# A hybrid decoder step on one core: the z and gate projections move to a first phase done by Strassen's algorithm, and the SSD decay is clamped with Relu

## The chip, the cores and the metric

The kernel runs on one core of one Trainium2 chip. The core has a matrix engine (TensorE, PE in the rows; its weight loads are listed apart as PEld), a vector engine (DVE), an activation engine (ACT), a general engine (POOL) and a sync engine (SP), which here issues every DMA. The five run their own instruction queues in order and meet through semaphores. The metric is the device time of one launch in microseconds. A difference of 0.2% or less is what a measurement of this kernel can't tell from no change.

## The reference

One layer of a hybrid decoder, for 2048 prompt tokens and 64 sample tokens (8 sequences of 8), in float32. Cut to what matters here:

```python
h = rms_norm(x, norm_w)                               # (tokens, 1024)
q, k, v, z_a, z_s, xbc, dt, g = split(h @ w_in)       # 1024, 256, 256, 1024, 2048, 3072, 32, 2*1024 columns
o_a = window_attention(rope(norm(q)), rope(norm(k)), v, sinks)
a_cs = cumsum(dt * A); seg = a_cs[l] - a_cs[s]
Lm = exp(where(causal, seg, -inf))                    # the SSD decay matrix, 128 x 128 per head and chunk
o_s = grouped_rms((ssd(conv(xbc), Lm) + D * x) * silu(z_s))
merged = sigmoid(g_a) * ((o_a * silu(z_a)) @ w_attn) + sigmoid(g_s) * (o_s @ w_ssd)
y = x + merged @ w_out
```

The columns of `w_in` that this case is about are z_a (1024), z_s (2048) and the two gates (2048): 5120 of the 9760 columns.

## The kernel before

Every large product is computed with float32 split into two float32r parts, high and low: the high part is a copy on ACT (line 147) and the low part is the difference on DVE (line 148). A product then takes three matmuls, high*high, high*low and low*high (`SPLIT3`). Weights come from DRAM as a `raw` tile of 256 columns (1 MB) and are split into `whl`; the normed input, transposed, is `hT`, eight tiles of 128 model dims. One such weight tile against 512 tokens is 2 x 8 x 3 = 48 matmuls of 128x512.

The tokens go in four blocks of 512 (`TB`). The 64 sample tokens ride along with one block: its columns are 576, done as two halves of 288 (`proj_w`, line 181).

There are three stages, one after the other, each with its own pools:

- `phase_t1`, the attention stage. `prep_first` and `prep_h` load x, norm it, transpose it and write both parts to DRAM (`h_d`). For every block: z_a tiles (`za_tile`, matmuls on line 168), k, v and q tiles (line 192), then 32 attention units over all blocks (scores on line 519, transposes on 536, the product with v on 547).
- `phase_s`, the SSD stage. For every block and each of four groups, `proj_group` computes B, C, x (with the convolution, lines 739 to 753) and z_s (lines 814 and 815, with silu). Then `ssd_group` goes through four chunks of 128 tokens: the decay `L` (eight DVE subtract-and-min on line 843, one Exp on line 844, a POOL product on line 845), the matmuls `py`, `st` and `po`, the state `H`, and at last the product with `zs`. The tiles of `proj_group` have two sets, so that it can run one group ahead.
- `phase_t2`, the output stage, in block order 3, 0, 1, 2. `gate` computes tanh of the gate projections (line 1175); `w_ssd`, `w_attn` and `w_out` follow. `phase_sa` and `phase_ss`, the sample tokens' attention and SSD (the loop over their states is on lines 1073 to 1085), are emitted into the first block; the third block, which carries the sample columns, needs their results.

The order on each engine isn't the order of the code: a scheduler that keeps its own estimate of the time interleaves the instructions, so projections stand between the steps of attention and of the SSD chunks. PE runs whatever order that gave, in order.

Of the kernel before, what the change touches and what calls it, by code (L numbers as in the profile page):

```python
# [9 lines left out]
F32 = mybir.dt.float32  # L10
# [65 lines left out]
def build(tc, nc, a, o, seq, phases=("T1", "S", "T2"), dbg=None):  # L76
# [14 lines left out]
    h_d = [[dt_(f"h_d{b}_{k}", [P, 4, 2, TB]) for k in range(KT // 4)] for b in range(NB)]  # L91
# [9 lines left out]
    zs_d = dt_("zs_d", [P, 16, 64])  # L101
# [4 lines left out]
    zss_d = dt_("zss_d", [P, 8, 64])  # L106

    def dump(name, t):
        if dbg is not None and name in dbg:
            SY.dma_start(dbg[name], t)  # L110
# [144 lines left out]
    def prep_first(xp, jp, zap, trp):  # L255
        rows = jp.tile([KT, P], F32, name="rows", tag="rows")
        zz = zap.tile([P, HG, TB], F32, name="zs", tag="zs").rearrange("p (i c) t -> p i (c t)", i=2)
        xts = [xp.tile([P, D], F32, name="xt", tag="xt") if tt < 2 else zz[:, tt - 2] for tt in range(NT)]
        for tt, xt in enumerate(xts):
            SY.dma_start(xt, a["x_prompt"][0, tt * P : (tt + 1) * P, :])  # L260
        SY.dma_start(rows, a["norm_w"][0].rearrange("(c p) -> c p", p=P))
        ips = trp.tile([P, KT], F32, name="tr", tag="tr")
        PE.transpose(ips, rows, ident[:KT, :KT])
        nw = jp.tile([P, KT], F32, name="nw", tag="nw")
        V.tensor_copy(nw, ips)
        for xt in xts:
            norm_x(xt, jp, None)
        hT = []
        for k in range(KT):
            tp = trp.tile([P, TB], F32, name="tr", tag="tr")  # L270
            for tt in range(NT):
                PE.transpose(tp[:, tt * P : (tt + 1) * P], xts[tt][:, k * P : (k + 1) * P], ident)
            ht = cur["h"].tile([P, 2, TB], F32R, name="hT", tag="hT")
            A.activation(ht[:, 0], tp, AF.Identity, bias=0.0, scale=nw[:, k : k + 1])
            V.scalar_tensor_tensor(
                out=ht[:, 1], in0=tp, scalar=nw[:, k : k + 1], in1=ht[:, 0].bitcast(F32),
                op0=ALU.mult, op1=ALU.subtract,
            )
            SY.dma_start(h_d[0][k // 4][:, k % 4], ht.bitcast(F32))
            hT.append(ht)  # L280
        return hT

    def prep_h(b, xp, jp, trp, nwb):
        for tt in range(NT):
            ts = slice(tt * P, (tt + 1) * P)
            xt = xp.tile([P, D], F32, name="xt", tag="xt")
            SY.dma_start(xt, a["x_prompt"][0, b * TB + tt * P : b * TB + (tt + 1) * P, :])
            norm_x(xt, jp, nwb)
            for kh in range(2):
                tp = trp.tile([P, 4, P], F32, name="tr", tag="tr")  # L290
                for k in range(4):
                    c = (4 * kh + k) * P
                    PE.transpose(tp[:, k], xt[:, c : c + P], ident)
                st = xp.tile([P, 2, 4, P], F32R, name="hst", tag="hst", bufs=2)
                split(st[:, 0], st[:, 1], tp)
                for i in range(2):
                    SY.dma_start(h_d[b][kh][:, :, i, ts], st[:, i].bitcast(F32))

    def prep_s(xp, jp, trp, nwb):
        xsm = xp.tile([64, D], F32, name="xsm", tag="xt")  # L300
        SY.dma_start(xsm, a["x_sample"].rearrange("b t d -> (b t) d"))
        norm_x(xsm, jp, nwb, 64)
        tp = trp.tile([P, KT, 64], F32, name="tr", tag="tr")
        for k in range(KT):
            PE.transpose(tp[:, k], xsm[:, k * P : (k + 1) * P], ident[:64, :64])
        V.tensor_copy(hs, tp)
# [65 lines left out]

    def phase_t1():
        with ExitStack() as es:
# [6 lines left out]
            jp = pool("jp", 1)  # L381
# [24 lines left out]

            def za_tile(b, pair, hgp, hT, zs):
                raw, hl = wtile(za_parts(pair, hgp))
                r5 = raw.rearrange("p k (v h d) -> p k v h d", v=2, h=2)
                for hgl in range(2):  # L410
                    ov = [hl[:, i, :, hgl * P : hgl * P + P].rearrange("p k (v d) -> p k v d", v=2) for i in range(2)]
                    split(ov[0], ov[1], r5[:, :, :, hgl, :])
                for hgl in range(2):
                    ps = mmp.tile([P, TB], F32, name="mm", tag="mm")
                    proj_cm(ps, hl, hgl * P, hT)
                    th = wk.tile([P, TB], F32, name="th", tag="th", bufs=1)
                    A.activation(th, ps, AF.Tanh, scale=0.5)
                    V.scalar_tensor_tensor(  # L418
                        out=zs[:, 2 * hgp + hgl], in0=th, scalar=1.0, in1=ps, op0=ALU.add, op1=ALU.mult
                    )  # L420
                if b == sb:
                    pss = mmp.tile([P, P], F32, name="mm", tag="mm")
                    proj_s(pss, raw, hs, views=lambda k, half: r5[:, k, :, half, :])
                    zt = wk.tile([P, P], F32, name="zt", tag="zt", bufs=1)
                    V.tensor_copy(zt, pss)
                    tp = trp.tile([P, P], F32, name="tr", tag="tr")
                    PE.transpose(tp, zt, ident)
                    A.activation(zt, tp, AF.Tanh, scale=0.5)
                    V.scalar_tensor_tensor(out=zt, in0=zt, scalar=1.0, in1=tp, op0=ALU.add, op1=ALU.mult)
                    ct = pair * 4 + hgp * 2  # L430
                    SY.dma_start(zss_d[:, ct : ct + 2].rearrange("p c t -> p (c t)"), zt)
# [138 lines left out]
            nxt = prep_first(xp, jp, zap, trp)  # L570
            for b in range(NB):
# [3 lines left out]
                for pair in range(2):  # L575
                    zs = zap.tile([P, HG, TB], F32, name="zs", tag="zs")
                    if pair == 0:
# [6 lines left out]
                    if pair == 0 and b + 1 < NB:  # L584
                        prep_h(b + 1, xp, jp, trp, nwb)
                        if b + 1 == sb:
                            prep_s(xp, jp, trp, nwb)
                    if pair == 1:
                        for hgp in range(2):
                            za_tile(b, pair, hgp, hT, zs)  # L590
# [5 lines left out]
    def phase_sa(oas):  # L596
        with ExitStack() as es:
# [11 lines left out]
            SY.dma_start(zss, zss_d)  # L609
# [96 lines left out]
    def phase_s():  # L706
        with ExitStack() as es:
# [3 lines left out]
            cur["whl"], cur["w"] = pool("whl2", 2), 256  # L711
            pst = pool("pst", 1)
# [70 lines left out]
            def proj_group(b, g, hT):  # L783
# [23 lines left out]
                for i in range(2):  # L807
                    c = 512 * g + 256 * i
                    _, hl = wload([(0, w_in[:, OFF_ZS + c : OFF_ZS + c + 256])])
                    st = sample_tile(smp)  # L810
                    for j in range(2):
                        th = cp.tile([P, TB], F32, name="th", tag="th")
                        for ps, lo, n in prompt_pieces(proj_w(mmp, hl, j * P, hT, smp), st[:, j] if smp else None):
                            A.activation(th[:, lo : lo + n], ps, AF.Tanh, scale=0.5)
                            V.scalar_tensor_tensor(
                                out=zs[:, 2 * i + j, lo : lo + n], in0=th[:, lo : lo + n], scalar=1.0, in1=ps,
                                op0=ALU.add, op1=ALU.mult,
                            )
# [498 lines left out]
```

## Time and profile before

| | |
|---|---|
| time, median of 3 runs | 3273.84 us (3271.09 to 3276.58) |
| span of the profiled execution | 3273.9 us, the same as the median to 0.1 us |
| PE busy | 3130.4 us, 96% |
| DVE, ACT, POOL busy | 2234.8, 1308.2, 1045.0 us |
| attention stage | about 0 to 790 us |
| SSD stage | about 790 to 2063 us |
| output stage | about 2063 to 3274 us |

The profiled execution has no time of its own beside its span, from the first to the last instruction. Busy time on PE counts a matmul from its start to its modelled end; matmuls overlap, so the mean duration of one (396 ns for 512 columns) is longer than the distance from one to the next. Where a group is busy without a gap, its busy time divided by its count is what one matmul costs.

### The profile page before, as it was taken

The page shows a single profiled execution, that of the slowest core. Times are in us where ns is not written, and L with a number is a line of the kernel's source. Part 1 is how long each engine was busy: PE and PEld are TensorE (multiplying, and loading weights), DVE is VectorE, ACT ScalarE, POOL GpSimd, SP SyncE. Part 2 cuts the span into 40 slices and gives each one's busy share as a digit, 9 for nine tenths or more (in the row PEclk, how much of TensorE's full clock was granted, in tenths as well). Part 3 has the DMA queues.
Part 4 walks back from the last instruction along what each step waited for, and adds up shares of the span by engine and source line. Part 5 has one row for each costly group of instructions (what it writes and reads, how often), then busy time and mean ns, then how long its engine had stood idle before and what let it go on. Part 6 is the DMA issues. An engine that isn't in the chain of part 4 may idle for free.

```text
span 3273.9 us, 49350 instructions
## 1 busy us (share of the span) xinstructions
PE 3130.4 (96%) x19038; PEld 2656.9 (81%) x19038; DVE 2234.8 (68%) x3777; ACT 1308.2 (40%) x2334; POOL 1045.0 (32%) x965
## 2 busy tenths in 40 slices
PE   6999999999989999998999999999999999999999
PEld 5978787878878877776777777788877799999888
DVE  3777768678887798989888898555555554334433
ACT  3555535456344344434444444332333333222322
POOL 1534343443445455556554555200211110000000
PEclk8999999999999999999999999999999999999999
DMA  6544425323433444444344433444764574345443
GB/s 210 156 134 124 128 73 169 106 70 124 130 122 110 154 125 135 126 156 133 116 143 155 127 118 119 154 141 117 229 184 142 131 226 147 97 135 168 132 116 101
DMA packets 472788, 448.76 MB, mean 137 GB/s; under 512 B 33808, under 2 KB 420520, under 8 KB 472504
## 3 DMA queue, kind: packets, MB, share of 16 engines
q1 hardware_dynamic: 472552, 445.60, 44.9%
q8 instruction: 150, 2.46, 0.3%
q14 instruction: 86, 0.70, 0.1%
HBM read 382.26 MB, written 65.35 MB: 137 GB/s over the span
## 4 chain that ended last, share of the span: by engine, by line
PE 63%; DVE 24%; DMA 5%; POOL 3%; issue 3%; ACT 2%; SPq 1%; DVEq 0%; ACTq 0%; POOLq 0%
PE mm L181 37%; PE mm L192 11%; DVE acc L748 5%; DVE L L843 5%; PE mm L168 5%; DVE whl L148 3%; PE tr L547 3%; PE sc L519 2%; POOL L L845 2%; DVE zs L885 1%; DMA v<-v_d 1%; PE tr L536 1%; DVE xT L882 1%; DVE H L879 1%; DMA hT<-h_d 1%
## 5 line engine op out<-in xcount | busy, mean ns | idle before, releaser
L181 PE MATMUL mm<-hT,whl 128*128 128x512 f32 (+1 forms) x6720 | 1353.7, 357 | 19.8 <-DMA hT<-h_d 9.9
L181 PEld LDWEIGHTS mm<-hT,whl 128*128 128x128 f32 x6720 | 1122.0, 190 | 194.0 <-issue 22.9
L148 DVE TENSOR_TENSOR whl<-raw,whl 128x2048 fp32r<-128x2048 f32 (+1 forms) x232 | 522.7, 2256 | 261.7 <-ACT whl L147 255.4
L181 PE MATMUL mm<-ot,whl 128*128 128x512 f32 (+1 forms) x2880 | 571.7, 356 | 1.2 <-DVE whl L148 0.8
L181 PEld LDWEIGHTS mm<-ot,whl 128*128 128x128 f32 x2880 | 476.1, 189 | 74.0 <-issue 5.7
L147 ACT CAST whl<-raw 128x2048 fp32r<-128x2048 f32 (+1 forms) x232 | 412.7, 1787 | 250.1 <-PE mm L181 133.9
L192 PE MATMUL mm<-whl,hT 128*128 128x256 f32 (+1 forms) x2304 | 305.6, 288 | 16.2 <-ACT whl L147 12.8
L192 PEld LDWEIGHTS mm<-whl,hT 128*128 128x128 f32 x2304 | 288.6, 190 | 24.4 <-ACT whl L147 13.0
L748 DVE SCALAR_TENSOR_TENSOR acc<-cr,cwb,acc 128x512 f32<-128x512 f32 x288 | 274.9, 960 | 10.4 <-ACT acc L743 5.0
L845 POOL TENSOR_TENSOR L<-L,cbm 128x1024 f32<-128x1024 f32 x64 | 200.2, 3138 | 115.3 <-DVE cbm L834 57.9
L192 PE MATMUL mm<-whl,ot 128*128 128x256 f32 (+1 forms) x1632 | 203.9, 284 | 0.0
L192 PEld LDWEIGHTS mm<-whl,ot 128*128 128x128 f32 (+1 forms) x1632 | 197.6, 188 | 5.3 <-issue 4.9
L168 PE MATMUL mm<-hT,whl 128*128 128x512 f32 x768 | 195.1, 403 | 6.0 <-DVE zs L418 3.7
L843 DVE TENSOR_SCALAR L<-AB,acs 128x128 f32<-128x128 f32 x512 | 192.0, 443 | 0.0
L168 PEld LDWEIGHTS mm<-hT,whl 128*128 128x128 f32 x768 | 142.6, 191 | 42.0 <-issue 5.2
L844 ACT ACTIVATE L<-L 128x1024 f32<-128x1024 f32 x64 | 67.8, 1062 | 187.8 <-DVE L L843 187.8
L365 ACT ACTIVATE s<-s,ng 128x128 f32<-128x128 f32 x256 | 100.0, 394 | 59.9 <-DVE ng L359 57.7
L147 ACT CAST ot<-v 128x512 fp32r<-128x512 f32 x96 | 59.0, 621 | 158.4 <-DVE v L1183 79.9
L752 ACT ACTIVATE th<-acc 128x512 f32<-128x512 f32 x96 | 60.6, 632 | 145.4 <-DVE acc L748 145.3
L869 POOL TENSOR_TENSOR ws<-wx,ws 128x512 fp32r<-128x512 f32 x64 | 102.5, 1601 | 44.4 <-ACT ws L868 44.4
L540 POOL TENSOR_TENSOR PT<-PT 128x512 f32<-128x512 f32 x60 | 78.2, 1308 | 92.6 <-DVE PT L539 78.9
L1183 DVE SCALAR_TENSOR_TENSOR v<-v,snw,rb 128x512 f32<-128x512 f32 x64 | 48.0, 770 | 84.7 <-DMA v<-v_d 84.7
(320 smaller groups left out, 3964.3 us busy)
## 6 DMA issues: line engine op xcount, KB each, us to landing
raw<-in_w_in_dram SPq DMA_DIRECT2D x120, 1024.0 KB
hT<-h_d SPq DMA_DIRECT2D x80, 512.0 KB
raw<-in_w_in_dram SPq DMA_DIRECT2D x64, 512.0 KB
AB<-ac_d SPq DMA_DIRECT2D x64, 512.0 KB
raw<-in_w_ssd_proj_dram SPq DMA_DIRECT2D x32, 1024.0 KB
v_d<-zs SPq DMA_DIRECT2D x16, 1024.0 KB
v<-v_d SPq DMA_DIRECT2D x64, 256.0 KB
raw<-in_w_attn_proj_dram SPq DMA_DIRECT2D x64, 256.0 KB
```

The costliest lines, as they stand in the source:

```text
L147: A.copy(hi, src)
L148: V.tensor_tensor(lo, src, hi.bitcast(F32), ALU.subtract)
L168: PE.matmul(ps, hl[:, x, k, c0 : c0 + P], ht[:, y, :], start=first and i == 0, stop=last and i == n - 1,)
L181: PE.matmul(ps, hl[:, x, k, c0 : c0 + P], ht[:, y, lo : lo + n], start=i == 0, stop=i == 3 * len(hT) - 1,)
L192: PE.matmul(ps, ht[:, x, tt * P : tt * P + m], hl[:, y, k, :n], start=i == 0, stop=i == 3 * len(hT) - 1,)
L365: A.activation(s[:, i, :width], s[:, i, :width], AF.Exp, bias=ng[:, i : i + 1], accum_out=den[:, i : i + 1])
L540: G.tensor_tensor(PT[:, 0], PT[:, 0], PT[:, 1], ALU.subtract)
L547: PE.matmul(po[64 * kvl : 64 * kvl + 64], vT[:, tt + w, kv * HD : (kv + 1) * HD], PTs[kvl][:, w], start=w == ws[0], stop=w == 1,)
L748: V.scalar_tensor_tensor(out=acc, in0=raw[:, k : k + TB], scalar=cwb[:, k, ct : ct + 1], in1=acc, op0=ALU.mult, op1=ALU.add)
L843: V.tensor_scalar(L[:, h], AB[:, h], acs[:, hc.start + h : hc.start + h + 1], 0.0, ALU.subtract, ALU.min)
L845: G.tensor_tensor(L, L, cbm[:, c].unsqueeze(1).to_broadcast([P, 8, P]), ALU.mult)
L869: G.tensor_tensor(ws[:, 1], wx, ws[:, 0].bitcast(F32), ALU.subtract)
```

## The change

A new `phase_p` comes first. It preps all 17 token tiles (16 of the prompt, one of the samples), writes the two parts `h_d` and also the unsplit `h32_d` to DRAM, and then computes all z and gate projections. The 2112 tokens are cut into three windows of 704 (`W2`), each of two halves of 352 (`H`). The 1024 model dims are cut in two halves of four tiles, and each weight tile of 256 columns in two of 128. So one unit (a weight tile and a window) is a 2x2 by 2x2 block product, done by the Strassen-Winograd form with 7 block products instead of 8: 7 x 4 x 3 = 84 matmuls of 128x352. There are 20 units per window and 60 in all. The sums of weights are made on POOL, those of tokens on DVE once per window, and the results are combined on ACT, DVE and POOL through three PSUM banks X, Y, Z. silu or tanh is applied there, and the result goes to DRAM (`za_o`, `zs_o`, `g_o`). The later stages load it where they computed it before. The early gates at the start of the output stage are gone, and so are the sample tokens' own z products.

The second part is in `ssd_group`: min(AB - acs, 0) followed by Exp becomes Relu(acs - AB) with Exp of its negative, both on ACT.

```diff
+    def prep_tile(xp, jp, trp, nwb, tt):
...
+            split(st[:, 0], st[:, 1], tp)
+            A.copy(s32, tp)
+            for i in range(2):
+                SY.dma_start(h_d[b][kh][:, :, i, lo : lo + n], st[:, i].bitcast(F32))
+            SY.dma_start(h32_d[b][:, 4 * kh : 4 * kh + 4, lo : lo + n], s32)
...
+    def phase_p():
...
+            ld = pool("ld0", 10)
+            op = pool("bop", 31)
+            wp = pool("wop", 8)
+            sp = pool("ws", 4)
+            ev = pool("ev", 2)
+            mmp = pool("mm0", 6, space=PSUM)
...
+            def h_ops(w):
...
+                for kt in range(4):
+                    r = {}
+                    for kh in range(2):
+                        k = kt + 4 * kh
+                        for th in range(2):
+                            t = ld.tile([P, H], F32, name="b", tag="b")
+                            o2 = None if (kh, th) == (0, 1) else op_tile(f"b{kh + 1}{th + 1}")
+                            for b, o_, n, d in pieces(w * W2 + th * H, w * W2 + th * H + H, TB):
+                                SY.dma_start(t[:, d : d + n], h32_d[b][:, k, o_ : o_ + n])
+                                if o2 is not None:
+                                    SY.dma_start(o2[:, :, d : d + n].bitcast(F32), h_d[b][kh][:, kt, :, o_ : o_ + n])
+                            r[kh, th] = t
...
+                    V.tensor_tensor(t3, r[1, 1], r[0, 1], ALU.subtract)
...
+                    for name, t in (("t2", t2), ("t1", t1), ("t3", t3), ("t4", t4)):
+                        o2 = op_tile(name)
+                        split(o2[:, 0], o2[:, 1], t)
...
+            def mms(ps, hl, ops, first):
+                i = 0
+                for k in range(4):
+                    for x, y in SPLIT3:
+                        PE.matmul(
+                            ps[:, :H], hl[:, x, k], ops[k][:, y], start=first and i == 0, stop=i == 11,
...
+                X, Y, Z = mm(), mm(), mm()
+                w1 = hl(a11)
+                s1 = add(a21, a22, ALU.add)
+                s2 = add(s1, a11, ALU.subtract)
+                mms(X, w1, ops["b11"], True)
+                c21 = evt("c21")
+                A.copy(c21, X[:, :H])
+                mms(Y, hl(s2), ops["t2"], True)
+                mms(X, hl(a12), ops["b21"], False)
...
+                emit(0, 0, X[:, :H])
+                c12 = evt("c12")
+                V.tensor_tensor(c12, Y[:, :H], c21, ALU.add)
+                mms(Z, hl(s1), ops["t1"], True)
+                z5 = evt("z5")
+                A.copy(z5, Z[:, :H])
+                mms(Y, hl(s3), ops["t3"], False)
+                c22 = evt("c22")
+                V.tensor_tensor(c22, Y[:, :H], c21, ALU.add)
+                mms(Z, hl(s4), ops["b22"], False)
+                G.tensor_tensor(c22, c22, z5, ALU.add)
+                emit(1, 1, c22)
+                mms(Y, hl(a22), ops["t4"], False)
...
+            def silu2(dst):
+                def emit(m, th, c):
+                    t = ev.tile([P, H], F32, name="th", tag="th")
+                    A.activation(t, c, AF.Tanh, scale=0.5)
+                    r = ev.tile([P, H], F32, name="r0", tag="r0") if (m, th) == (0, 0) else c
+                    V.scalar_tensor_tensor(out=r, in0=t, scalar=1.0, in1=c, op0=ALU.add, op1=ALU.mult)
+                    SY.dma_start(dst(m)[:, th * H : th * H + H], r)
...
+            for w in range(3):
+                ops = h_ops(w)
+                for i, u in enumerate(units(w, ops)):
+                    u()
+                    if w + 1 < 3 and i >= 4 and done <= ends[w + 1]:
+                        prep_tile(xp, jp, trp, nwb, done)
...
-            def za_tile(b, pair, hgp, hT, zs):
...
-                    if pair == 1:
-                        for hgp in range(2):
-                            za_tile(b, pair, hgp, hT, zs)
...
-                    _, hl = wload([(0, w_in[:, OFF_ZS + c : OFF_ZS + c + 256])])
...
+                for w, o_, n, d in pieces(b * TB, (b + 1) * TB, W2):
+                    SY.dma_start(zs[:, :, d : d + n], zs_o[w][g][:, :, o_ : o_ + n])
...
-                        V.tensor_scalar(L[:, h], AB[:, h], acs[:, hc.start + h : hc.start + h + 1], 0.0, ALU.subtract, ALU.min)
-                    A.activation(L, L, AF.Exp)
+                        A.activation(L[:, h], AB[:, h], AF.Relu, scale=-1.0, bias=acs[:, hc.start + h : hc.start + h + 1])
+                    A.activation(L, L, AF.Exp, scale=-1.0)
...
-            def gate(j, off, hT, smp, ts=None, mmp=mmp):
...
+            def gate_load(j, off, b, smp):
...
+                        SY.dma_start(t[:, d : d + n], g_o[w][off + 2 * j + c][:, o_ : o_ + n])
...
-                early = early_gates(b, hT)
```

On PE the program began with the prep of the first block and the first z_a tile mixed in with it (line 272 the transposes of x and 168 the z_a matmuls):

```order
L263 MATMUL tr<-cst,rows 128x8
L272 MATMUL tr<-cst,xt 128x128 x6
L272 MATMUL tr<-cst,zs 128x128 x6
L168 MATMUL mm<-hT,whl 128x512 x2
L272 MATMUL tr<-cst,xt 128x128 x2
L272 MATMUL tr<-cst,zs 128x128 x2
L168 MATMUL mm<-hT,whl 128x512 x8
```

Now it begins with the transposes of x (line 278), and the products of the first units (line 405) come in between them:

```order
L278 MATMUL tr<-cst,xt 128x128 x40
L405 MATMUL mm<-ot,wa 128x352 x3
L278 MATMUL tr<-cst,xt 128x128 x28
L405 MATMUL mm<-ot,wa 128x352 x9
L278 MATMUL tr<-cst,xt 128x128 x4
L405 MATMUL mm<-ot,wa 128x352 x6
```

The first matmul of a projection stood behind 12 transposes of x; now the first three stand behind 40, the next nine behind 28 more, and 96 of the 136 are past before the products run on without them.

On PE in the attention stage, the second half of block 0 had z_a matmuls (line 168) between scores (519), transposes of the weights of attention (536) and products with v (547):

```order
L168 MATMUL mm<-hT,whl 128x512 x28
L519 MATMUL sc<-KTT,qT 128x256 x2
L536 MATMUL tr<-cst,s 128x128 x4
L519 MATMUL sc<-KTT,qT 128x256 x2
L168 MATMUL mm<-hT,whl 128x512
L547 MATMUL tr<-PT,vT 64x512
L168 MATMUL mm<-hT,whl 128x512 x2
L536 MATMUL tr<-cst,s 128x128 x4
L519 MATMUL sc<-KTT,qT 128x256 x4
L168 MATMUL mm<-hT,whl 128x512 x7
```

The same place now (scores are line 649, transposes 666, products with v 677, and v's projection 202):

```order
L666 MATMUL tr<-cst,s 128x128 x3
L649 MATMUL sc<-KTT,qT 128x256 x12
L666 MATMUL tr<-cst,s 128x128
L677 MATMUL tr<-PT,vT 64x512
L666 MATMUL tr<-cst,s 128x128 x3
L649 MATMUL sc<-KTT,qT 128x256 x8
L677 MATMUL tr<-PT,vT 64x512
L649 MATMUL sc<-KTT,qT 128x256 x12
L666 MATMUL tr<-cst,s 128x128 x4
L649 MATMUL sc<-KTT,qT 128x256 x8
```

The z_a matmuls are gone from between the steps of attention, and nothing stands in their place there.

On ACT in the SSD stage, block 0, the decay was one Exp (line 844) among the copies that free PSUM for the convolution (742 and 743) and the split of the states' inputs (868):

```order
L868 CAST ws<-wx 128x512
L844 ACTIVATE L<-L 128x1024
L742 COPY cr<-mm 128x288
L743 ACTIVATE acc<-mm,cwb 128x288
L742 COPY cr<-mm 128x224
L743 ACTIVATE acc<-mm,cwb 128x224
```

Now eight Relu (line 953) stand ahead of the Exp (954), the others being 978, 864 and 865:

```order
L953 ACTIVATE L<-AB,acs 128x128 x8
L954 ACTIVATE L<-L 128x1024
L978 CAST ws<-wx 128x512
L864 COPY cr<-mm 128x288
L865 ACTIVATE acc<-mm,cwb 128x288
L953 ACTIVATE L<-AB,acs 128x128 x8
L864 COPY cr<-mm 128x224
L865 ACTIVATE acc<-mm,cwb 128x224
```

The eight instructions of each chunk have moved from DVE's queue to ACT's, in one piece, ahead of copies that PE's PSUM tiles wait for.

## Rows read from the trace of the kernel before

**Rows 1.** The page: span, busy time by engine, the chain by engine

```profile
span 3273.9 us, 49350 instructions
...
PE 3130.4 (96%) x19038; PEld 2656.9 (81%) x19038; DVE 2234.8 (68%) x3777; ACT 1308.2 (40%) x2334; POOL 1045.0 (32%) x965
...
PE 63%; DVE 24%; DMA 5%; POOL 3%; issue 3%; ACT 2%; SPq 1%; DVEq 0%; ACTq 0%; POOLq 0%
```

**Rows 2.** Stretches: the three stages (busy us and instructions by engine, clock, DMA)

```profile
core 0: us, PE busy (x) PEld busy (x) DVE busy (x) ACT busy (x) POOL busy (x), PEclk, DMA share, GB/s
0.00:790.00 790.00, 749.35 (x4986) 623.73 (x4987) 558.28 (x1161) 394.93 (x1060) 299.34 (x367) 0.98 0.43 132
790.00:2063.00 1273.00, 1178.14 (x6854) 985.82 (x6852) 1104.85 (x1682) 546.97 (x761) 671.25 (x536) 0.98 0.42 130
2063.00:3274.00 1211.00, 1202.90 (x7200) 1047.33 (x7200) 571.63 (x936) 366.32 (x514) 74.36 (x62) 1.00 0.50 148
```

**Rows 3.** Groups by line and form, PE: busy us, mean ns, idle before

```profile
L181 PE MATMUL mm<-hT,whl 128*128 128x512 f32 x4032 | 972.6, 395 | 12.8 <-DMA hT<-h_d 7.4 <-DVE whl L148 3.8 <-ACT t L1175 1.1
...
L181 PE MATMUL mm<-hT,whl 128*128 128x288 f32 x2688 | 381.2, 300 | 7.0 <-ACT acc L743 4.2 <-DMA hT<-h_d 2.5
...
L168 PE MATMUL mm<-hT,whl 128*128 128x512 f32 x768 | 195.1, 403 | 6.0 <-DVE zs L418 3.7 <-ACT hT L274 2.3
...
L203 PE MATMUL mm<-raw,hs 128*64 128x128 f32 x320 | 25.1, 281 | 0.0
...
L293 PE MATMUL tr<-cst,xt 128*128 128x128 f32 x96 | 14.1, 273 | 0.0
```

**Rows 4.** Timeline, PE: matmuls back to back, first at 512 columns

```profile
1367.57 15.14 PE L181 MATMUL mm<-hT,whl 128*128 128x512 f32 x66
```

**Rows 5.** Timeline, PE: the same at 256 columns

```profile
48.01 11.57 PE L192 MATMUL mm<-whl,hT 128*128 128x256 f32 x96
```

**Rows 6.** DMA of the first 60 us: all packets, and the main queue's share

```profile
DMA packets 13630, 11.04 MB, mean 184 GB/s; under 512 B 5813, under 2 KB 12093, under 8 KB 13629
...
q1 hardware_dynamic: 13629, 11.02, 60.9%
```

**Rows 7.** Stretches: the first 50 us

```profile
0.00:50.00 50.00, 34.26 (x146) 26.92 (x147) 19.22 (x29) 18.55 (x26) 3.54 (x13) 0.97 0.72 221
```

**Rows 8.** Issue of DMAs of h on SP: ns min/median/max

```profile
L312 SPq DMA_DIRECT2D hT<-h_d x80: 319/417/1616, 176.7 to 2937.0; - x80
```

**Rows 9.** Groups by line and form, DVE, ACT and POOL

```profile
L148 DVE TENSOR_TENSOR whl<-raw,whl 128x2048 fp32r<-128x2048 f32 x200 | 483.3, 2417 | 253.9 <-ACT whl L147 247.6 <-DMA raw<-in_w_attn_proj_dram 6.0
...
L843 DVE TENSOR_SCALAR L<-AB,acs 128x128 f32<-128x128 f32 x512 | 192.0, 443 | 0.0
...
L365 ACT ACTIVATE s<-s,ng 128x128 f32<-128x128 f32 x256 | 100.0, 394 | 59.9 <-DVE ng L359 57.7 <-DVE den L367 1.8
...
L844 ACT ACTIVATE L<-L 128x1024 f32<-128x1024 f32 x64 | 67.8, 1062 | 187.8 <-DVE L L843 187.8
L148 DVE TENSOR_TENSOR ot<-v,ot 128x512 fp32r<-128x512 f32 x96 | 65.1, 688 | 38.7 <-ACT ot L147 38.3
...
L147 ACT CAST ot<-v 128x512 fp32r<-128x512 f32 x96 | 59.0, 621 | 158.4 <-DVE v L1183 79.9 <-DMA v<-oa_d 36.6 <-PE mm L192 21.3
...
L540 POOL TENSOR_TENSOR PT<-PT 128x512 f32<-128x512 f32 x60 | 78.2, 1308 | 92.6 <-DVE PT L539 78.9 <-DVE den L367 4.8 <-DVE den L366 4.2
...
L148 DVE TENSOR_TENSOR whl<-raw,whl 128x1024 fp32r<-128x1024 f32 x32 | 39.3, 1252 | 7.8 <-ACT whl L147 7.8
...
L815 DVE SCALAR_TENSOR_TENSOR zs<-th,mm 128x512 f32<-128x512 f32 x48 | 32.8, 684 | 47.4 <-ACT th L814 47.1
```

**Rows 10.** One line: the sample states' product on POOL, ns min/median/max, first and last start

```profile
L1083 POOL TENSOR_TENSOR h<-h,dec x32: 1035/1042/3132, 2310.4 to 2652.6; 128x512 f32<-128x512 f32 x32
```

**Rows 11.** Stretches: the end of the SSD stage

```profile
2020.00:2040.00 20.00, 16.98 (x95) 13.69 (x94) 15.33 (x16) 5.29 (x5) 14.36 (x7) 0.91 0.38 113
2040.00:2060.00 20.00, 14.06 (x102) 11.16 (x101) 19.31 (x28) 8.68 (x11) 16.41 (x11) 0.83 0.33 99
```

More of the change, by code (lines that the diff above doesn't have):

```diff
@@ L89, in ct_ @@
         return const.tile(shape, dtype, name=name, tag=name)
-    h_d = [[dt_(f"h_d{b}_{k}", [P, 4, 2, TB]) for k in range(KT // 4)] for b in range(NB)]
+    W2 = (seq + 64) // 3
+    H = W2 // 2
+    h_d = [[dt_(f"h_d{b}_{k}", [P, 4, 2, TB if b < NB else 64]) for k in range(KT // 4)] for b in range(NB + 1)]
+    h32_d = [dt_(f"h32_d{b}", [P, KT, TB if b < NB else 64]) for b in range(NB + 1)]
+    zs_o = [[dt_(f"zs_o{w}_{g}", [P, 4, W2]) for g in range(4)] for w in range(3)]
+    za_o = [[dt_(f"za_o{w}_{p}", [P, 4, W2]) for p in range(2)] for w in range(3)]
+    g_o = [[dt_(f"g_o{w}_{i}", [P, W2]) for i in range(16)] for w in range(3)]
     oa_d = [[dt_(f"oa_d{b}_{p}", [4, P, TB]) for p in range(2)] for b in range(NB)]
@@ L105, in build, with pieces @@
     qks_d = dt_("qks_d", [P, 640])
[L106 to L110, printed above, removed]
+    def pieces(a, b, size):
+        out, t = [], a
+        while t < b:
+            k = t // size
+            n = min(b, (k + 1) * size) - t
+            out.append((k, t - k * size, n, t - a))
+            t += n
+        return out
     cst = ct_("cst", [P, C_END])
@@ L253, in norm_x @@
             V.scalar_tensor_tensor(out=xt, in0=xt, scalar=st[:, 2:3], in1=nwb[:n], op0=ALU.mult, op1=ALU.mult)
[L255 to L297, printed above, removed]
@@ L405, in sample_cols @@
                     SY.dma_start(d, src)
-            def za_tile(b, pair, hgp, hT, zs):
[L408 to L431, printed above, removed]
             def k_tile(b, hT, tab):
@@ L608, in phase_sa @@
             zss = one.tile([P, 8, 64], F32, name="zss")
-            SY.dma_start(zss, zss_d)
+            for p in range(2):
+                SY.dma_start(zss[:, 4 * p : 4 * p + 4], za_o[2][p][:, :, W2 - 64 :])
             tab0 = one.tile([P, 80], F32, name="tab0s")
@@ L806, in proj_group @@
                         SY.dma_start(xs_d[:, 4 * g + 2 * i : 4 * g + 2 * i + 2], st)
-                for i in range(2):
-                    c = 512 * g + 256 * i
-                    _, hl = wload([(0, w_in[:, OFF_ZS + c : OFF_ZS + c + 256])])
[L810 to L818, printed above, removed]
-                    if smp:
-                        SY.dma_start(zs_d[:, 4 * g + 2 * i : 4 * g + 2 * i + 2], st)
+                for w, o_, n, d in pieces(b * TB, (b + 1) * TB, W2):
+                    SY.dma_start(zs[:, :, d : d + n], zs_o[w][g][:, :, o_ : o_ + n])
                 return xT, BT, CT, zs
@@ L912, in phase_s @@
                     stats(b, g)
-            cur["hT"] = hT
             for g in range(4):
@@ L1016, in phase_ss @@
                 zg = wk.tile([P, 4, 64], F32, name="zg", tag="zg", bufs=1)
-                A.activation(zg, zst, AF.Tanh, scale=0.5)
-                V.scalar_tensor_tensor(out=zg, in0=zg, scalar=1.0, in1=zst, op0=ALU.add, op1=ALU.mult)
+                SY.dma_start(zg, zs_o[2][g][:, :, W2 - 64 :])
                 EB = wk.tile([P, 4, 64], F32, name="EB", tag="EB")
@@ L1191, in phase_t2 @@
             sb = order[min(2, NB - 1)]
-            def early_gates(b, hT):
-                out = []
-                for j in range(3 if b == order[0] else 1):
-                    ts = op.tile([P, 2, TS], F32R, name="ot", tag="ot") if j else None
-                    out.append(gate(j, OFF_GS, hT, b == sb, ts, mmps[0] if b == order[0] else mmp))
-                return out
             for b in order:
```

155 lines of the change are left out of this document (119 added, 36 removed).

## The prediction, made before the changed kernel was run

> **What bounds the kernel now.** I read the page first. PE is busy 96% of the span, and PE makes up 63% of the chain that ended last, DVE 24% [rows 1]. That is an average over three stages, so the view by stretches comes next. There PE is busy 749 of 790 us in the attention stage, 1178 of 1273 in the SSD stage and 1203 of 1211 in the output stage [rows 2]. DVE stands at 558, 1105 and 572 [rows 2]. The reader is to see two things. PE bounds every stage; it idles only 41, 95 and 8 us. But in the SSD stage DVE is 87% busy beside it, so work taken from PE alone would soon bring out DVE there. POOL (671 us) has more room, ACT (547) the most [rows 2]. The groups by form then give the price of a matmul: busy time over count is 972.6/4032 = 0.241 us at 512 columns and 381.2/2688 = 0.142 us at 288 [rows 3]. The timeline gives it for an unbroken run: 15.14/66 = 0.229 us at 512 [rows 4] and 11.57/96 = 0.1205 us at 256 [rows 5]. The difference of the two views is short stalls.
>
> All sums are against the profiled execution's 3273.9 us, which is the median of the runs to 0.1 us.
>
> **What PE loses and gains.** z_s is 8 weight tiles: in three blocks 3 x 8 x 48 = 1152 matmuls of 512, in the sample block 8 x 96 = 768 of 288. At the prices above that is 278 + 109 = 387 us, from the SSD stage. The gates are 8 tiles with the same counts: 387 us, from the output stage. z_a is 195 us (its own group), and the sample tokens' z_a is 4 of the 10 weight tiles of line 203, 10 us of 25.1 [rows 3]; both leave the attention stage. Together 979 us go.
>
> What comes is 60 units x 84 = 5040 matmuls of 352 columns, a width that no row shows. Between the two prices by groups (0.142 at 288, 0.241 at 512) it is 0.142 + 64/224 x 0.099 = 0.170 us; between the two unbroken runs 0.1205 + 96/256 x 0.109 = 0.161 us. I take 0.170, since the new units have as many waits as the old tiles: 857 us. So PE's work falls by 979 - 857 = 122 us, 3.7% of the span. Columns fall by an eighth, but there are more matmuls than before, each with its fixed part.
>
> The Trainium skill (TensorE: Matmul & The Clock Gate, "Back-to-back issue gap") puts the gap of warm matmuls at N/2.4 + 2.5 ns, thus 216 at 512 and 109 at 256. This trace's unbroken runs show 229 and 120.5 ns, about 12 more at both widths [rows 4, 5], so here the fixed part is larger than the page's, and it weighs against more and narrower matmuls. By the page alone 979 would be 851 and 857 would be 752, a fall of 99 us, an estimate that the sum doesn't use.
>
> **The new phase: 997 us.** Its 857 us of matmuls are one term.
>
> Its start is the second. Nothing can be multiplied in earnest until window 0's operands are read back from DRAM. In SP's order 12 tiles of x, 40 writes of `h_d`, 19 of `h32_d` (256 KB each), all of the window's operand loads (7.2 MB), some weights (3 MB), both cache copies and the constants stand ahead of the last such load or among them: 6 + 15.5 + 7 + 3 + 3, about 34 MB. In the first 60 us of before 11 MB moved at 184 GB/s with the engines 60.9% busy, so 302 GB/s when full [rows 6]: 34 MB take 114 us. Some 80 products (14 us) get done between the transposes, so I take 100 us lost. Before, the first 50 us lost only 16 [rows 7]. Bounds: 50, if the transfers run well above 302; 140, if the short rows of the writes slow them.
>
> The third is the change of window. There are 31 operand tiles and a window needs 28, so most loads of the next window wait for the last unit's products, and its first product needs a tile of each of the four `kt`. It is 40 to 56 DMAs; at 0.417 us to issue one [rows 8], 48 take 20 us. Two changes cost 40 us; bounds 10 and 60.
>
> Other engines per unit, with 352-column operations at the price of 512: DVE 7 x 0.688 for the low parts, 4 x 0.684 to combine, and 4 x 0.684 silu in 36 of 60 units, 9.2 us; ACT 7 x 0.621 and six more of about 0.6, 8 us; POOL 5 x 1.308, 6.5 us [rows 9]. PE needs 84 x 0.170 = 14.3. These are hidden beside PE if they keep step: the third, fifth and seventh products of a unit go into a bank that ACT or DVE must first have read, with one or two products (2 to 4 us) between. If that cover fails, the units run at the pace of DVE (below).
>
> **The attention stage: 590 us (790 before).** PE keeps 749 - 195 - 10 - 19 for the prep's transposes (14.1 for 96 of 128 [rows 3]) = 525 us. DVE loses the z_a splits (39.3), 32 silu at 0.684 (22) and some prep [rows 9], and keeps 497 at most, 95% of PE's work where it had 75%. The order shows runs of attention steps without projections between them, so PE will wait for the softmax there. Idle was 41 us, 16 of it at the start [rows 2, 7]; I take 65. Bounds 25 and 115.
>
> **The SSD stage: 906 us (1273).** PE keeps 1178 - 387 = 791. DVE loses `L` (192.0), 32 splits at 2.417 (77) and 64 silu at 0.684 (44) [rows 9], and keeps 792. So the clamp's move is what stops DVE from being far behind PE. On ACT the 512 Relu cost at most what line 365 takes for an Exp of the same size with a bias, 0.394 us, and at least an eighth of line 844's 1.062, 0.133 [rows 9]; I take the first, nearest in form: 202 us, which brings ACT to 749 at most. POOL stays at 671. Four engines then lie between 671 and 792, and each chunk passes through all of them. Before, PE was at 92.5% with DVE at 87%; I take 87% for both now, 115 us idle. At 92.5% it would be 855, at 80% 990. The end adds to it: in its last 40 us PE was busy 31 [rows 11], partly with gates that are gone.
>
> **The output stage: 860 us (1211).** PE keeps 1203 - 387 = 816. The sample states' 32 steps took from 2310 to 2653 us [rows 10] and PE never waited, since between the first and the last step its order had 963 matmuls of 512 and 444 of 256: 232 + 54 = 286 us at the prices above. Now it has 576, 96 of 288 and 480 of 256: 139 + 14 + 58 = 211. If the steps need their 342 us anyway, PE waits 75 us; if PE's order held them back, none. I take the middle, 36, and the old 8. The gate loads from DRAM replace larger weight loads.
>
> **The sum.** 997 + 590 + 906 + 860 = 3353 us, 2.4% slower. PE does 122 us less, but its idle time goes from 144 to 364, of which the new phase's 140 come from DRAM round trips that didn't exist.
>
> **Rivals.**
> First, PE stays the bound as it was, and this is faster. The mechanism: the units run like the unbroken stretches, and the scheduler finds enough cover in each stage. The new phase is then 813 + 100 + 40 = 953, attention 525 + 25, SSD 791 + 95, output 816 + 8: 3213 us. For it speaks that PE was at 92.5% beside a DVE at 87%, and that DVE loses as large a part in the SSD stage as PE does. Against it stands the fill of attention and of the sample steps that is gone from PE's order. It decides from an idle time outside the new phase's start and changes of window of at most 144 us at the group price, or 188 at the unbroken one.
>
> Second, the new phase is bound by DVE and POOL in turn. POOL's line 1083 takes 1.035 us at best, 3.132 at worst for the same operation [rows 10], so something holds it up for the length of other instructions. If POOL's 6.5 us and DVE's 9.2 add up, a unit takes 15.7 us, 60 take 942, and the total is 3438 us. For it: the units put POOL sums of weights right beside DVE differences. Against it: only some of DVE's instructions read two SBUF operands, and weights are prepared a unit ahead.
>
> The Trainium skill (SBUF — State Buffer, "Who interferes with whom") says that a DVE instruction with two SBUF inputs contends with a POOL instruction that reads SBUF. The range of durations of line 1083 agrees with that; the second rival is what it would do here.
>
> **How the numbers follow.** The forecast gets 0.53, the first rival 0.27, the second 0.20. The likeliest case's own range is 3270 to 3430 (start 50 to 140, the three stages half way to their bounds). With the rivals it reaches from 3205 to 3470. 0.2% of the time, 7 us, is about what a measurement can tell from no change: the first rival is faster (0.27), 0.05 of the forecast's chance lies within 7 us, and the rest, 0.68, is slower.
>
> **What the profile will show.** The stretches of the four phases against 997, 590, 906 and 860. The first dense run of line 405 at about 110 us. A gap on PE of 15 to 20 us at each change of window. Line 405's busy time over 5040, against 0.161 and 0.170, with the releasers named in the idle before it. Relu at 0.39 us against 0.13. DVE and PE both near 87% in the SSD stage. Gaps on PE at the sample steps. I am wrong if the new phase takes under 930 us, or if the SSD stage keeps PE above 92%.

## The result and the profile after

The changed kernel takes 3503.2 us (median of 4 runs, 3502.2 to 3508.1) against 3272.8 us for the kernel before, run beside it: 1.071 times as long, 95% interval 1.069 to 1.072. That is slower, as forecast, but 150 us above the forecast and 33 above its range.

Page of the changed kernel: the span, busy time by engine with its share, and the granted clock in 40 slices (compare [rows 1]).

```profile
span 3500.4 us, 53316 instructions
...
PE 3117.3 (89%) x19337; PEld 2725.2 (78%) x19337; DVE 2463.9 (70%) x3923; ACT 1624.0 (46%) x3406; POOL 1426.1 (41%) x1265
...
PEclk9899999999999999999999999899889999979999
```

PE was busy 96% and is busy 89%. It was to lose 122 us of work and lost 13; its idle time went from 144 to 383 us. The stretches say where, against [rows 2]; the first two are the new phase (its start apart), then attention, the SSD stage and the output stage.

```profile
core 0: us, PE busy (x) PEld busy (x) DVE busy (x) ACT busy (x) POOL busy (x), PEclk, DMA share, GB/s
0.00:137.00 137.00, 36.53 (x131) 27.63 (x132) 52.19 (x71) 48.46 (x90) 22.20 (x37) 0.92 0.85 254
137.00:983.00 846.00, 822.98 (x5047) 813.00 (x5045) 563.38 (x888) 407.15 (x843) 395.94 (x302) 0.99 0.53 163
983.00:1585.00 602.00, 541.98 (x3858) 447.51 (x3859) 452.21 (x1087) 306.76 (x947) 269.34 (x333) 0.97 0.33 106
1585.00:2570.00 985.00, 845.65 (x4991) 690.70 (x4991) 906.52 (x992) 595.08 (x1140) 673.39 (x532) 0.93 0.49 153
2570.00:3500.00 930.00, 870.12 (x5315) 746.38 (x5313) 489.61 (x887) 266.50 (x389) 65.23 (x62) 0.96 0.55 160
```

| | new phase | attention | SSD | output |
|---|---|---|---|---|
| before | | 790 | 1273 | 1211 |
| forecast | 997 | 590 | 906 | 860 |
| after | 983 | 602 | 985 | 930 |

The new phase and attention came out within 14 us. The miss is 79 us in the SSD stage (55 of PE's busy time and 24 of its idle time) and 70 in the output stage (54 and 16). In the SSD stage DVE is busy 907 of 985 us, where 792 had been summed. Its groups there (busy us, mean ns, idle before):

```profile
L870 DVE SCALAR_TENSOR_TENSOR acc<-cr,cwb,acc 128x512 f32<-128x512 f32 x284 | 314.0, 1116 | 6.5 <-ACT acc L865 4.8
L158 DVE TENSOR_TENSOR whl<-raw,whl 128x2048 fp32r<-128x2048 f32 x47 | 117.5, 2499 | 6.3 <-ACT whl L157 6.3
L995 DVE TENSOR_TENSOR zs<-zs,xT 128x512 f32<-128x512 f32 x64 | 81.7, 1276 | 6.6 <-POOL xT L994 6.6
L875 DVE SCALAR_TENSOR_TENSOR xT<-th,acc 128x512 f32<-128x512 f32 x64 | 66.8, 1053 | 7.0 <-ACT th L874 6.6
L992 DVE TENSOR_TENSOR xT<-py,xT 128x512 f32<-128x512 f32 x64 | 43.5, 679 | 5.1 <-PE py L976 4.1 <-POOL xT L991 0.9
```

All but the second work on 128x512. `L992`, with one operand in PSUM, takes 0.68 us; `acc`, `zs` and `xT`, with both in SBUF, take 1.05 to 1.28 (before, by the same view: 0.96, 0.99 and 0.74). The same stage's list of waits (who waited for whom: us in total, times, longest) shows who suffers:

```profile
ACT th L874 <- DVE acc L870: 149.2, 61, 7.7
POOL cr L861 <- DVE acc L870: 103.2, 50, 9.0
...
PE st L1005 <- DVE thl L1001: 28.6, 11, 4.1
```

The others wait mostly for DVE, DVE for nobody long. Of PE's 139 us of idle time in the stage 113 end on a DVE instruction and 9 on one of POOL; before, 75 of 95 ended on DVE. What stretches its instructions stands in two timelines of the same 5 us (start, us, instruction), first DVE:

```profile
1703.01 0.68 DVE L971 TENSOR_TENSOR dx<-tr,dt 128x512 f32<-128x512 f32 x1
1703.61 0.68 DVE L972 TENSOR_TENSOR wx<-tr,wd 128x512 f32<-128x512 f32 x1
1704.21 2.81 DVE L995 TENSOR_TENSOR zs<-zs,xT 128x512 f32<-128x512 f32 x1
```

Then POOL:

```profile
1703.10 1.04 POOL L991 TENSOR_TENSOR xT<-xT,Dcol 128x512 f32<-128x512 f32 x1
1704.10 2.37 POOL L955 TENSOR_TENSOR L<-L,cbm 128x1024 f32<-128x1024 f32 x1
1706.43 1.74 POOL L979 TENSOR_TENSOR ws<-wx,ws 128x512 fp32r<-128x512 f32 x1
```

`dx` and `wx` read PSUM and run 0.68 us beside POOL's `L991`. `zs` starts 0.1 us after POOL's `L955`, and ends at 1707.02, 0.55 us after `L955` does: it waits for all of `L955`, then runs. It is so throughout the stage. Of its 443 instructions of `acc`, `zs` and line 875, 178 took over 0.9 us, and every one of these ended 0.52 to 0.58 us after a POOL instruction that computes on tensors. Before, it was 102 of 429.

The Relu took what was forecast, 0.391 us each, and their busy time, overlaps counted once, is 157 us where 202 had been summed:

```profile
L953 ACT ACTIVATE L<-AB,acs 128x128 f32<-128x128 f32 x512 | 157.1, 391 | 20.6 <-PE py L976 6.5
```

### The profile page after: what moved, and what is told of

Same layout as the page of the kernel before. It is cut to its first block, busy times and chain, and to the rows that moved or that the text cites. A ratio compares the mean times of both kernels' runs of the same rounds, so it can differ in the third digit from the quotient of the medians.

```text
span 3500.4 us, 53316 instructions
## 1 busy us (share of the span) xinstructions
PE 3117.3 (89%) x19337; PEld 2725.2 (78%) x19337; DVE 2463.9 (70%) x3923; ACT 1624.0 (46%) x3406; POOL 1426.1 (41%) x1265
## 5 line engine op out<-in xcount | busy, mean ns | idle before, releaser
L405 PE MATMUL mm<-ot,wa 128*128 128x352 f32 x5040 | 833.7, 327 | 35.2 <-DMA ot<-h_d 11.7
L405 PEld LDWEIGHTS mm<-ot,wa 128*128 128x128 f32 x5040 | 818.6, 191 | 47.1 <-DMA ot<-h_d 14.0
L191 PE MATMUL mm<-hT,whl 128*128 128x512 f32 (+1 forms) x2880 | 609.9, 364 | 17.2 <-DMA hT<-h_d 8.9
L191 PEld LDWEIGHTS mm<-hT,whl 128*128 128x128 f32 x2880 | 486.1, 193 | 93.2 <-DMA hT<-h_d 9.8
L158 DVE TENSOR_TENSOR whl<-raw,whl 128x2048 fp32r<-128x2048 f32 x136 | 320.9, 2361 | 88.3 <-ACT whl L157 87.5
L157 ACT CAST whl<-raw 128x2048 fp32r<-128x2048 f32 x136 | 258.9, 1906 | 163.8 <-PE mm L191 75.6
L426 POOL TENSOR_TENSOR s<-raw 128x512 f32<-128x512 f32 x120 | 174.4, 1454 | 393.6 <-DMA raw<-in_w_in_dram 305.4
L158 DVE TENSOR_TENSOR wa<-s,wa 128x512 fp32r<-128x512 f32 x240 | 193.9, 815 | 45.5 <-ACT wa L157 44.5
L955 POOL TENSOR_TENSOR L<-L,cbm 128x1024 f32<-128x1024 f32 x64 | 186.0, 2915 | 41.8 <-ACT L L954 34.8
L157 ACT CAST wa<-s 128x512 fp32r<-128x512 f32 x240 | 147.2, 616 | 47.5 <-PE mm L405 44.8
L953 ACT ACTIVATE L<-AB,acs 128x128 f32<-128x128 f32 x512 | 157.1, 391 | 20.6 <-PE py L976 6.5
```

What stands on the lines that cost most here:

```text
L157: A.copy(hi, src)
L158: V.tensor_tensor(lo, src, hi.bitcast(F32), ALU.subtract)
L191: PE.matmul(ps, hl[:, x, k, c0 : c0 + P], ht[:, y, lo : lo + n], start=i == 0, stop=i == 3 * len(hT) - 1,)
L405: PE.matmul(ps[:, :H], hl[:, x, k], ops[k][:, y], start=first and i == 0, stop=i == 11, skip_group_check=not first,)
L426: G.tensor_tensor(t, x, y, alu)
L953: A.activation(L[:, h], AB[:, h], AF.Relu, scale=-1.0, bias=acs[:, hc.start + h : hc.start + h + 1])
```

## The experiments

Theory 1: in the SSD stage DVE and POOL exclude each other, and DVE becomes the bound. Rivals: ACT's Relu hold up the copies out of PSUM; PE's lower clock. Theory 2: in the output stage the sample states' steps lost their cover. Its rival: the miss is in my prices.

**The clamp back on DVE.** The changed kernel with

```
-  A.activation(L[:, h], AB[:, h], AF.Relu, scale=-1.0, bias=acs[...])
-  A.activation(L, L, AF.Exp, scale=-1.0)
+  V.tensor_scalar(L[:, h], AB[:, h], acs[...], 0.0, ALU.subtract, ALU.min)
+  A.activation(L, L, AF.Exp)
```

> The changed kernel with the decay's clamp back on DVE (512 subtract-min instructions, Exp as before); nothing else is undone. Theory 1 (DVE is the bound of the SSD stage, 906 of 985 us busy): DVE gets 512 x 0.443 = 227 us at most, 192 by its union in the trace of before, so the stage goes from 985 to about 1160 us and the total from 3503 to about 3680 us (3640 to 3730). Rival 1 (ACT's 512 Relu stand ahead of the copies out of PSUM and hold PE up): ACT loses 157 us of work, the stage is 985 us or less, the total 3503 us or less. Rival 2 (PE's lower granted clock, 0.93 in that stage, sets its time): within 20 us of 3503.

3575.8 us, 1.093 [1.091, 1.095]: 72 us more than the change, not 177. SSD stage, then one DVE group:

```profile
1585.00:2660.00 1075.00, 879.58 (x5044) 712.18 (x5043) 1026.94 (x1516) 457.63 (x636) 687.74 (x537) 0.90 0.45 142
```

```profile
L870 DVE SCALAR_TENSOR_TENSOR acc<-cr,cwb,acc 128x512 f32<-128x512 f32 x286 | 287.8, 1024 | 7.2 <-ACT acc L865 6.2
```

DVE got 197 us more work but only 120 more busy time, and it fills 96% of the stage. The other two-operand instructions grew shorter: POOL was 64% busy instead of 68, and 130 of them, not 178, took over 0.9 us. Both rivals fall: without the Relu on ACT the stage is 90 us longer. Only the size was off, because I added DVE's work to stretched instructions.

**The clamp alone.** The same edit the other way round on the kernel before.

> The kernel before with the clamp moved from DVE to ACT and nothing else. Theory 1: DVE falls from 1105 to about 913 us in an SSD stage that PE bounds at 1178, so only PE's 95 us of idle time there can shrink: the total is 3215 us (3190 to 3250), and DVE's work, not PE's, was part of what PE waited for. Rival 1 (ACT's Relu hold up the copies out of PSUM): 3274 us or more. Theory 1 also gives the Relu at 0.391 us each.

3219.5 us, 0.984 [0.982, 0.985]; the middle of the expectation. SSD stage:

```profile
790.00:2005.00 1215.00, 1169.71 (x6857) 982.92 (x6856) 962.87 (x1175) 695.33 (x1276) 689.02 (x536) 0.99 0.43 137
```

PE's idle time in the stage fell from 95 to 45 us. So this part of the change is a gain, and the rest of it costs about 284 us. One part of the expectation missed: DVE fell to 963 us and not to 913. With the clamp on ACT its two-operand instructions already grew longer in this stage, at POOL 57% busy: `acc` from 0.96 to 1.00 us, `zs` from 0.99 to 1.25, and 133 of 430 took over 0.9 us.

**POOL that reads nothing.** In the changed kernel:

```
-  G.tensor_tensor(L, L, cbm[:, c]..., ALU.mult)
+  for _ in range(3):
+      G.memset(L, 0.0)
   (likewise ws[:, 1] 3 fills, hd 2, u * Dcol 3, u + EB 3)
```

> The changed kernel with the five large POOL operations of each SSD chunk (product with cbm, low part of ws, decayed state, product with D, sum with EB) replaced by two or three fills of the same output: POOL stays busy at the same places, but reads nothing from SBUF; those five products and sums are left out of what is computed. Theory 1, second half (DVE's instructions with two SBUF inputs are stretched by POOL's instructions that read SBUF): acc falls from 1.12 us to 0.69 to 0.75, zs from 1.28 to about 0.70, xT from 1.05 to about 0.70; DVE's busy time in the stage falls from 906 to about 700 us, PE bounds it, stage about 880 us, total about 3400 us (3370 to 3430). Rival (they are longer for another reason, such as DMA traffic or ACT's reads): durations within 5%, total within 20 us of 3503.

3360.5 us, 1.026 [1.024, 1.029]: 143 us less than the change. The stage, two DVE groups and a POOL group:

```profile
1585.00:2432.00 847.00, 812.67 (x5039) 675.68 (x5038) 692.62 (x1002) 593.15 (x1144) 626.87 (x1101) 0.98 0.59 180
```

```profile
L870 DVE SCALAR_TENSOR_TENSOR acc<-cr,cwb,acc 128x512 f32<-128x512 f32 x285 | 212.6, 750 | 20.4 <-ACT acc L865 13.0 <-POOL xT L995 2.7 <-POOL xT L999 2.3
...
L1000 DVE TENSOR_TENSOR zs<-zs,xT 128x512 f32<-128x512 f32 x64 | 44.0, 687 | 33.1 <-POOL xT L999 33.1
```

```profile
L956 POOL MEMSET L<- 128x1024 f32 x192 | 183.0, 954 | 21.4 <-ACT L L954 14.0 <-DMA AB<-ac_d 5.3
```

POOL is busy 627 us, 74% of the stage (68% in the changed kernel), and DVE's two-operand instructions are back close to their shortest: `acc` 0.75, `zs` 0.69. Only 3 of 445 took over 0.9 us. DVE's busy time fell by 214 us and the stage by 138, until PE bound it at 96%. PE's granted clock, a mean over its two levels (1.2 and 2.4 GHz), rose from 0.93 to 0.98, and its busy time fell by 33 us with the same matmuls: here the low clock followed PE's waits and was not what set the stage. The Trainium skill (SBUF — State Buffer, "Who interferes with whom") gives the rule, an exclusive lock between a DVE instruction with two SBUF inputs and a POOL instruction that reads SBUF. The timeline and this run agree: 1.28 us with POOL's reads, 0.69 without. The fills also drop POOL's dependence on `cbm`, `H` and `EB`, so a part of the 138 us may be shorter chains; PE's direct waits for POOL, which could show them, were only 9 us in the changed kernel.

**Four buffers for the states of the steps.**

```
-  h0 = wk.tile([P, 4, P], F32, name="h0", tag="h0", bufs=2)
+  h0 = wk.tile([P, 4, P], F32, name="h0", tag="h0", bufs=4)
```

> The changed kernel with four buffers instead of two for the states loaded in the sample states' 32 steps. Theory 2 (the steps' own chain, load, product, sum, store, two at a time, lasts longer than the matmuls that now lie beside it, and PE idles 34 us of 3000 to 3110 us): with four in flight the chain is shorter, the output stage goes from 930 to about 880 us and the total to about 3455 us (3440 to 3480). Rival (the steps are held where PE's order put them, and more buffers change nothing): within 10 us of 3503.

3481.5 us, 1.063 [1.061, 1.065]: 22 us less, between the two. The output stage took 901 us:

```profile
2580.00:3481.00 901.00, 856.42 (x5309) 741.33 (x5307) 488.69 (x885) 263.88 (x386) 68.66 (x62) 0.98 0.56 165
```

Loads are a part of it: PE's waits for the loaded states, 9.7 us in the changed kernel, are gone. From the first to the last of POOL's products the steps take 293 us where they took 317, and these products still wait 104 us in all for PE's transposes (124 before), so where PE's order puts these is likely to hold the steps back too.

**Without the steps, after and before.** In both kernels

```
-  for q in range(2):
+  for q in range(0):
```

> The changed kernel without the sample states' 32 steps (their loads, transposes, products, sums and stores are left out; the rest of the sample part stays). Theory 2 (the steps outlast the matmuls that lie beside them, and PE idles 34 us of 3000 to 3110 at a clock of 0.75): more goes than the steps' own PE work, which is about 1.5 us a step, 48 us in all: total about 3400 us (3385 to 3420). Rival (the stage's 70 us too much are elsewhere: a price of the removed gates that I set too high, loads at its start): only the steps' own work goes, as it does without them in the kernel before: about 3455 us.

> The kernel before without the same 32 steps. There PE never waited in the output stage, so only the steps' own PE work can go, about 48 us: total about 3223 us (3210 to 3240). Theory 2 expects the fall here to be about half of that of the changed kernel; its rival expects the same fall in both.

After: 3399.3 us, 1.039 [1.037, 1.040], a fall of 104. Before: 3213.6 us, 0.982 [0.981, 0.984], a fall of 58 or 59. In the kernel before, PE idles 8 us in the output stage with the steps and 6 without them, so the 58 us are about their own work. Then the steps cost 45 us beyond it after the change and nothing before: theory 2 in direction. The output stages, after and before, without steps:

```profile
2581.00:3397.00 816.00, 791.72 (x4948) 704.50 (x4946) 451.87 (x787) 239.07 (x337) 9.99 (x14) 0.99 0.55 160
```

```profile
2065.00:3211.00 1146.00, 1139.64 (x6842) 1016.76 (x6840) 534.03 (x837) 339.68 (x463) 10.38 (x14) 1.00 0.47 141
```

The gates of that stage in the kernel before without steps:

```profile
L181 PE MATMUL mm<-hT,whl 128*128 128x512 f32 (+1 forms) x1866 | 363.2, 352 | 0.0
```

1146 - 363 = 783, so 33 us more than that remain even without steps, 18 of them idle. Waits of PE in the changed kernel without steps, where the same view of the kernel before lists 3.6 us:

```profile
PE mm L191 <- ACT whl L157: 7.9, 4, 3.3
PE mm L191 <- DVE whl L158: 7.2, 6, 2.7
PE mm L191 <- ACT ot L157: 5.1, 5, 2.5
```

So the gates had also covered waits for the splitting of weights and operands, 20 us in this list.

**Plain products in the new phase.**

```
-  X, Y, Z = mm(), mm(), mm()        (7 products, 4 sums of weights, 5 of results)
+  for m in range(2):
+      for th in range(2):
+          X = mm()
+          for kh in range(2):
+              mms(X, ws_[m][kh], ops[f"b{kh + 1}{th + 1}"], kh == 0)
+          emit(m, th, X[:, :H])
   (no t1 to t4, no h32_d)
```

> The changed kernel with the units of the new phase by plain products of the same four quarters: 8 instead of 7 (96 matmuls of 352 columns a unit, 5760 in all), no sums of weights, of operands or of products, and no f32 copy of the transposed x in DRAM. If PE alone sets the phase's pace, 720 more matmuls at 0.1654 us cost 119 us, less some 20 us for the shorter start and the operands of the next window loaded early: total about 3600 us (3580 to 3620), and Strassen's saving is about 100 us, too little to pay for the phase's start. Rival (the sums on DVE, ACT and POOL hold PE up within the units): a matmul is nearer to 0.161 and the total 3560 us or less.

3547.8 us, 1.084 [1.083, 1.086]: 45 us more than with Strassen, so the rival. Matmuls of the phase in the changed kernel and in this one, then this one's start and the rest of the phase:

```profile
L405 PE MATMUL mm<-ot,wa 128*128 128x352 f32 x5040 | 833.7, 327 | 35.2 <-DMA ot<-h_d 11.7
L387 PE MATMUL mm<-ot,wa 128*128 128x352 f32 x5760 | 931.0, 323 | 8.0 <-DMA ot<-h_d 8.0
```

```profile
0.00:103.00 103.00, 23.05 (x80) 16.22 (x80) 24.93 (x37) 24.09 (x42) 6.78 (x21) 1.00 0.74 228
103.00:1033.00 930.00, 929.50 (x5816) 928.78 (x5816) 256.24 (x407) 259.09 (x509) 6.80 (x18) 1.00 0.45 142
```

931.0/5760 is 0.1616 us a matmul, with Strassen 833.7/5040 = 0.1654. Strassen saves 97 us of matmul time, then gives back 43 in waits: PE idles 100 us at the start against 80, and 23 us within the phase against almost none. Taken in steps, in shares of the time before: the clamp is worth -1.6%, the move of the projections into their own phase +10.1%, Strassen in that phase -1.3%. The order of the steps counts: taken last, the clamp was worth 72 us, taken first 52.

**Less work for POOL.** In the changed kernel, and in the kernel before with the clamp alone:

```
-  G.tensor_tensor(u, u, Dcol[:, 4 * g : 4 * g + 4]..., ALU.mult)
+  for i in range(4):
+      A.activation(u[:, i], u[:, i], AF.Identity, bias=0.0, scale=Dcol[:, 4 * g + i : ...])
```

> The changed kernel with the product of u and D (64 POOL instructions of 128x512, 90 us busy in the SSD stage) made by 256 ACT instructions of 128x128. Theory 1: DVE's two-input instructions wait for the end of POOL's that read SBUF; the 213 us that DVE lost in the stage (906 less 693 with fills) fall by about 90/554, POOL's part that goes, thus 34 us; the stage goes from 985 to about 950, the total from 3503 to about 3470 us (3445 to 3485). Rival (what sets the stage is the length of the chain through all four engines, and ACT, with 256 x 0.391 = 100 us more, gets in its way): 3503 us or more.

> The kernel before with the clamp on ACT (3219.5 us) and the product of u and D on ACT too. There PE is busy 1170 of 1215 us in the SSD stage, so theory 1 expects at most part of the 45 us of idle time back: about 3210 us (3200 to 3220). Rival (ACT, at 695 + 100 us, delays the copies out of PSUM that PE waits for): 3225 us or more.

Changed kernel: 3486.4 us, 1.066 [1.064, 1.067], 17 us less, where 33 were expected. SSD stage:

```profile
1585.00:2555.00 970.00, 848.12 (x5030) 696.38 (x5029) 863.93 (x999) 666.97 (x1401) 583.69 (x473) 0.94 0.50 156
```

DVE's busy time fell by 43 us, somewhat more than the 34 expected, but the stage only by 15: at 89% DVE seems no longer alone in setting it. PE's waits for ACT's `acc` rose from 8 to 15 us, and those for POOL's `L` from none to 11. Kernel before with both edits: 3189.3 us, 0.974 [0.973, 0.976], faster than either kernel, by 30 us more than the clamp alone where 10 were expected:

```profile
790.00:1978.00 1188.00, 1164.78 (x6855) 982.05 (x6855) 943.86 (x1171) 768.12 (x1532) 596.66 (x472) 0.99 0.44 140
```

PE's idle time in the stage fell to 23 us.

## Why the prediction came out as it did

Right: slower, and a part of why. The cost of the projections' own phase, the lost cover in the attention and output stages and the clamp as a gain are in the runs. The forecast made it 2.4% slower and it is 7.1%, and the larger part of the difference has a cause that the sum did not hold.

- The new phase: 983 us for 997, by errors that cancel. A matmul cost 0.1654 us, between the two prices given (834 us for 857). The start took 137 us with 36.5 of PE work, 100 lost as summed, and for the reason given: at 254 GB/s the DMA moved 35 MB in it, where 34 had been counted. The two changes of window, priced at 40 us, show gaps of 1.8 and 0.4 us that wait for operands: the next window's loads came early enough. In their place stand 23 us of idle time spread over the units, and 26 us of PE work beside line 405, mostly the transposes, which the sum had left out (PE is busy 860 us in all).
- Attention: 602 for 590. PE kept 542 for 525, the idle time is 60 for 65.
- **The step that failed is DVE's work in the SSD stage: it loses `L`, 32 splits and 64 silu "and keeps 792".** It kept 907. The instructions that stay were priced at what they took beside a POOL that was 53% busy. With the clamp moved and the stage shortened, POOL was 68% busy, and DVE's two-operand instructions waited for it more often: 178 of them instead of 102. The sum should have held that 115 us of DVE. The clamp's move alone brings 50 of it, in a stage of 1215 us; the rest comes with the shorter stage. I had seen the lock, and put it on the new phase alone, as the second rival. There PE stayed at 97% although DVE and POOL together were busy 959 us in 846, so the two did not add up. In the SSD stage it decided the time: with POOL's reads gone the stage takes 847 us, less than the 855 of my best bound.
- ACT was not the trouble: 595 us for "at most 749".
- **The output stage: 930 for 860.** The gates of that stage were priced by the mean of both stages, 387 us, but 48 of their 1152 wide matmuls ran before it, and the narrow ones took 0.135 us each instead of 0.142; its own rows give 371 with the steps in place: 16 us. The steps' exposed cost is 45 us where I took the middle, 36: 9 us. The other 45 are waits that the gates had covered (8 us of idle time were forecast) and busy time at a lower clock where PE waits (granted clock 0.61 from 3050 to 3110 us, where PE is busy 37 of 60 us); the run without steps shows 33 us of it, 18 idle. How the rest divides stays open.
- The sum of PE, -122 us, became -13, chiefly because PE was busy 55 us longer than forecast in the SSD stage and 54 in the output stage. In the SSD stage 33 us of that vanish with POOL's reads, together with the low clock.
- What was to prove me wrong, the new phase under 930 or PE above 92% in the SSD stage, did not happen; the range was broken from the other side. Its upper end allowed for the second rival, at 3438, and for the likeliest case with each stage half way to its bound. The SSD stage went nearly all the way (985 of 990), and the output stage passed its bound (816 + 75 + 8 = 899) by 31 us. The likeliest case's range was also narrower than its own terms: 3353 with 40 for the start, 25, 42 and 20 for the half ways is 3480 and not 3430, above even the 3470 of the whole range.

## What to carry to other kernels

When a stage gets shorter, the density of every other engine's work in it rises; price DVE's instructions with two SBUF operands by what POOL's reading instructions will then occupy beside them, not by their means of before. POOL's busy share alone does not give that price: it was 53, 57, 64 and 68% before, with the clamp alone, with the clamp back and after, but `zs` took 0.99, 1.25, 0.98 and 1.28 us, short with the clamp on DVE and long with it on ACT. So the order of instructions on the two engines counts too. Matmuls that bound a stage also cover its waits: what moves them elsewhere pays for each cover that it takes away. Here the whole move cost 10% of the time, its start of 100 us without products included, and a saving of an eighth of the products came to 1.3%. Edits that take work off the pair of DVE and POOL and put it on ACT, the least busy of the three there before (547 us), gave 2.6% with no move at all.

## What the runs showed of the hardware

- A DVE instruction of 128x512 with two SBUF operands takes 0.68 to 0.75 us alone and up to 2.9 beside POOL; those with a PSUM operand had means of 0.68 us in the SSD stage, before and after, and at most 0.71 with the fills. Two or three POOL fills in place of one POOL product, about as long in sum, left the two-operand instructions at 0.68 to 0.75.
- It is not the number of operands alone: the cast of `thl` (128x512, one SBUF operand) went from 0.48 us before to 1.00 after the change, and was still at 0.65 beside fills that read nothing. After the change, and with the fills:

```profile
L1001 DVE CAST thl<-xT 128x512 fp32r<-128x512 f32 x15 | 15.0, 999 | 0.1
```

```profile
L1006 DVE CAST thl<-xT 128x512 fp32r<-128x512 f32 x15 | 9.7, 646 | 0.1
```

- A matmul of 352 columns in the unbroken phase of plain products, at clock 1.00, comes every 0.1616 us, on the line between the 0.1205 at 256 and 0.229 at 512 of [rows 4, 5].
